# Mixer A's softmax in pairs of banks, the scaling on ScalarE, and PSUM banks by mixer

## The chip, the core and the metric

The kernel runs on one core of a Trainium2 chip. A core has a matrix engine (PE, with its weight loads shown apart as PEld), a vector engine (DVE), a scalar engine for activations (ACT), a general one (POOL) and one that only issues transfers (SP). Each works through its own queue in order. PE writes into PSUM, which has eight banks of 512 float32 per partition; DVE and ACT read it there. The metric is the device time of one execution in microseconds, the median of the runs. Times inside an execution come from the profile of one of them, counted from its first instruction.

## What is computed

One layer of a diffusion backbone on 640 tokens (128 context, 512 latent), model width 1024. Cut to what matters:

```python
h = RMSNorm(x) * (1 + scale1) + shift1
aq, ak, av, bq, bk, bv, ga, gb = split(h @ w_in)      # 34 tiles of 128 columns
# mixer A: 8 query heads, 2 key heads, all 512 latent + 128 cached keys
p = softmax(q @ k.T / 8)                              # [512 queries, 640 keys] per head
a = p @ v
# mixer B: 8 heads, a window of 384 or 512 keys per 128 queries, with a bias
b = softmax(q @ k.T / 8 + bias) @ v
x = x + gate1 * ((sigmoid(ga) * (a @ w_br_a) + sigmoid(gb) * (b @ w_br_b)) @ w_out)
x = x + gate2 * (relu(h2 @ w1) ** 2 @ w2)
```

The context queries of each mixer read the 128 context keys alone. Products are made in three parts (`wh*xh + wh*xl + wl*xh`, L339 to L341), with each operand split into a high and a low half of its bits.

## The kernel before

Feature tiles lie on the 128 partitions, tokens along the free dimension, in halves of 320. The program has stages: the first norm with the first three tiles of the input projection (to 57 us), attention of mixer A and then of mixer B with the other input tiles laid between as filler (to 345 us), then merge, output projection and MLP.

**Attention** is a list of units (L951 to L956): per pair of heads `HeadA`, `HeadA`, `CtxPair`, four times, and then the same for mixer B. `attention` (L921) goes through it in steps. A step takes one transposed key tile `T(i)` of the unit before, one score tile `S(i)` of the present unit, and the product with the values (`pv`) that the last step's `T` left. The rest of a budget of `STEP` = 2050 ns goes to the filler (`F.spend`, L875), whose pieces are three matmuls, booked at 400 ns.

- `HeadA.S` (L629) makes the scores of 128 queries and 640 keys as two products of 320 into two banks. For each DVE finds the maximum (L641); a minimum of the two negated maxima follows (L642), then two exponentials on ACT with their sums (L644), the sum of the sums (L645), a reciprocal (L618) and the scaling of the 640 columns on DVE (L619).
- `HeadA.T` (L650) transposes a key tile of the four query tiles into one bank (L653); ACT and DVE split it (L606, L607), and `pv` multiplies it with the values (L660, L661).
- `fill_tile` (L788) multiplies one input tile for the first half of the tokens and then for the second, into a bank each (`pg`), which ACT copies out (L813, or L553 for mixer B's queries). Mixer A's later queries go through a norm (L527) and a rotation.
- The weights are copied to their high part by ACT (L301), and POOL or DVE subtracts it to get the low part (L302), 128x1024 in one instruction.

**PSUM** is one pool for the whole program (L69): two banks `g` for products, three `s` for scores, two `t` for transposes, one `o` for the product with the values.

**What sets the order.** Outside of marked stretches a list scheduler places the instructions on each engine. It goes by the program's order, and where an engine has nothing ready it pulls later work ahead, as far as the tiles it needs (banks among them) are free. So the number of banks decides how much filler can run ahead.

Of the kernel before, what the change touches and what calls it, by code (L numbers as in the profile page):

```python
# [10 lines left out]
F32 = mybir.dt.float32  # L11
# [46 lines left out]
def trunk_layer(ctx: ExitStack, tc: tile.TileContext, xT, small_in, wmodA, wmodB, tabs, cacheK, cacheV, bias,  # L58
# [10 lines left out]
    pp = ctx.enter_context(tc.tile_pool(name="pp", bufs=1, space=bass.MemoryType.PSUM))  # L69
# [27 lines left out]

    def ps_g():
        return pp.tile([P, 512], F32, tag="g", bufs=2, name="pg")

    def ps_s():
        return pp.tile([P, 512], F32, tag="s", bufs=3, name="pss")

    def ps_t():
        return pp.tile([P, 512], F32, tag="t", bufs=2, name="pt")

    def ps_o():
        return pp.tile([P, 512], F32, tag="o", bufs=1, name="po")
# [94 lines left out]
    later = []                                       # work put off until the next product  # L203
# [10 lines left out]
    class Weights:  # L214
        def __init__(self):
            self.order = list(w_order())
            self.pos = {k: i for i, (k, _) in enumerate(self.order)}
            self.loads = []                              # (key, source, number of the pair's tile)
# [31 lines left out]
        def block(self, name, i):  # L250
            """one operand of the seven products, [hi | lo]"""
# [37 lines left out]
        def conv(self):  # L289
# [4 lines left out]
            else:  # L294
# [7 lines left out]
                (nc.gpsimd if key in WPOOLSET else DVE).tensor_sub(lo, st, r32(hi))  # L302
# [52 lines left out]
    def modulate(todo, rstd, h, between=None):  # L355
        """for each (dst, x, s, sh): dst = the two parts of x * s * rstd + sh"""
# [22 lines left out]
    def warm(n):  # L379
        """keeps the tensor engine's clock up while it has to wait"""  # L380
# [3 lines left out]
    def mod_product(f, q):  # L384
        """silu(c) @ w_mod for the shift and scale of feature tile f; partial sums in four column groups"""
# [34 lines left out]
    def first_gemm(f, i, part):  # L420
        """the products of h's part with one weight tile; both parts of the tile take the high part of h"""
# [105 lines left out]
    def qk_norm(raw, g, h, bank=ps_g, src=None, buf=None):  # L527
# [23 lines left out]
    def q_part(qs, e, sl, src):  # L551
        """hi of src / 8 in the head's own partitions, lo in the other ones"""
# [4 lines left out]
    def qa_part(qs, e, raw, eng):  # L557
        """the same of mixer A's queries, whose gain holds the 1 / 8"""
# [3 lines left out]
    def k_part(k, e, dst, src, eng=None):  # L562
        """own half of the stacks k[0] = [hi; hi], k[1] = [lo; lo]"""
# [4 lines left out]
    def k_both(k, e, dst, src):  # L568
        """both halves of the stacks, the other one by the engines as well"""
# [13 lines left out]
    def v_stack(raw, cvp, bank=ps_g):  # L583
        """per key tile (ctx, lat 0..3, cache): [hi 64 | lo 64] of each of the pair's heads; in two pieces"""
# [25 lines left out]
    def combine(dst, ps, n):  # L610
        """dst (64 partitions, float32) = ps[0:64] + ps[64:128]"""
# [4 lines left out]
    def normalise(p, sm):  # L616
        rc = small("rc", 1)
        DVE.reciprocal(rc, sm)  # L618
        DVE.tensor_scalar(p, p, rc, None, op0=OP.mult)  # L619

    class HeadA:
        """512 latent queries of one head of mixer A on the latent and the cached keys"""
# [6 lines left out]
        def S(self, qt):  # L629
# [4 lines left out]
            ps = [ps_s(), ps_s()]  # L634
            p = u("pa")
            n2, s2, nm, sm = small("n2"), small("s2"), small("nm", 1), small("sm", 1)
            for j in range(2):
                c = slice(P + j * HT, P + (j + 1) * HT)
                PE.matmul(ps[j][:, :HT], q, kh[:, c], start=True, stop=False)
                PE.matmul(ps[j][:, :HT], q, kl[:, c], start=False, stop=True)  # L640
                DVE.tensor_reduce(n2[:, j:j + 1], ps[j][:, :HT], axis=AX.X, op=OP.max, negate=True)  # L641
            DVE.tensor_tensor(nm, n2[:, 0:1], n2[:, 1:2], op=OP.min)  # L642
            for j in range(2):
                ACT.activation(p[:, HALVES[j]], ps[j][:, :HT], AF.Exp, bias=nm, accum_out=s2[:, j:j + 1])  # L644
            DVE.tensor_add(sm, s2[:, 0:1], s2[:, 1:2])  # L645
# [21 lines left out]
    BQ = ((P, 384, 1, 256), (P, 512, 0, 0), (384, 512, 0, 128), (512, 384, 1, 0))   # keys, width, bias tile, columns  # L667
# [704 lines left out]
```

## Time and profile before

| what | value |
|---|---|
| median of 3 runs | 1002.95 us (1001.87 to 1005.6) |
| span of the profiled execution | 1001.3 us |
| HBM traffic over the span | 104 GB/s |
| scores of mixer A, first and last start | 75.0 and 213.8 us |
| scores of mixer B, first start | 216.8 us |
| weight loads of PE busy | 91% of the span |

The profiled execution's total time is not listed beside its span. A row of a group gives the line, engine, operation, what is written and read, count, busy time, the mean of one in ns, and the idle time before with what ended it. A row of stretches gives start and end, length, and then for each engine the busy time and the number of instructions, last the clock granted to PE (1.00 is full), the transfers' share and GB/s. A row of waits gives who waited, for whom, the total, how often, and the longest.

### The profile page before, as it was taken

What the parts mean: (1) busy time and instruction counts of PE and PEld (TensorE: products, weight loads), DVE (VectorE), ACT (ScalarE), POOL (GpSimd) and SP (SyncE); (2) the same over time, 40 slices, a digit from 0 to 9 for tenths busy, and PEclk for the clock granted to TensorE, in tenths of its full rate; (3) what the DMA queues carried; (4) which work ended last, traced back from release to release, by engine and by line L of the source; (5) the groups of instructions that cost most, each with busy time, mean ns of one, the idle gap of its engine ahead of it and who ended that gap; (6) DMA issues with size and microseconds to landing.
All of it is one profiled execution on the core that took longest, in us unless ns stands there. A gap on an engine that the chain in (4) does not pass through costs nothing.

```text
span 1001.3 us, 16554 instructions
## 1 busy us (share of the span) xinstructions
PE 955.0 (95%) x6317; PEld 908.8 (91%) x6317; DVE 705.0 (70%) x1576; ACT 517.6 (52%) x1117; POOL 173.5 (17%) x154
## 2 busy tenths in 40 slices
PE   7979899999899999999999999999999999999996
PEld 5778778978889999999998899999999999999896
DVE  4479898788866789788587677778733884368644
ACT  5475676668655564654324564237611662156542
POOL 0352232212231011201132100012200220012100
PEclk9999899999999999999999899999999999999999
DMA  9942101312543455556742153212320233120302
GB/s 347 208 172 69 31 25 44 77 43 77 135 111 103 133 160 189 181 169 185 224 126 81 47 164 110 85 43 84 106 78 28 85 106 88 60 79 29 126 22 105
DMA packets 34767, 108.47 MB, mean 108 GB/s; under 512 B 4320, under 2 KB 8032, under 8 KB 34688
## 3 DMA queue, kind: packets, MB, share of 16 engines
q1 hardware_dynamic: 27072, 82.63, 26.5%
q0 software_dynamic: 6464, 23.47, 8.1%
q10 hardware_dynamic: 1152, 1.31, 0.4%
q8 instruction: 49, 0.80, 0.3%
q14 instruction: 30, 0.25, 0.1%
HBM read 99.14 MB, written 4.60 MB: 104 GB/s over the span
## 4 chain that ended last, share of the span: by engine, by line
PE 65%; DVE 15%; ACT 8%; issue 3%; DMA 1%; POOL 0%; ACTq 0%; DVEq 0%; POOLq 0%; SPq 0%
PE pg L339 7%; PE pg L340 7%; PE pg L341 7%; PE pss L340 7%; PE pss L341 7%; PE pss L339 6%; PE pt L339 4%; PE pt L341 4%; PE pt L340 4%; DVE sr L260 3%; ACT wb L280 2%; PE pt L653 1%; PE pt L710 1%; DMA wst<-w 1%; DVE n L641 1%
## 5 line engine op out<-in xcount | busy, mean ns | idle before, releaser
L301 ACT ACTIVATE wh<-wst 128x1024 fp32r<-128x1024 f32 x84 | 88.8, 1057 | 112.4 <-PE pg L340 37.9
L302 DVE TENSOR_TENSOR wl<-wst,wh 128x1024 fp32r<-128x1024 f32 x53 | 64.8, 1223 | 67.5 <-ACT wh L301 67.4
L302 POOL TENSOR_TENSOR wl<-wst,wh 128x1024 fp32r<-128x1024 f32 x31 | 75.1, 2423 | 160.0 <-ACT wh L301 151.5
L992 DVE SCALAR_TENSOR_TENSOR mt<-wmt,cb 128x512 f32<-128x512 f32 x128 | 81.4, 686 | 0.0
L281 POOL TENSOR_TENSOR wb<-wst,wb 128x512 fp32r<-128x512 f32 x24 | 31.7, 1322 | 263.4 <-ACT wb L280 226.6
L339 PE MATMUL pss<-hidh,wh 128*128 128x320 f32 x216 | 67.0, 310 | 0.7 <-ACT hidh L1143 0.7
L340 PE MATMUL pss<-hidl,wh 128*128 128x320 f32 x216 | 67.0, 310 | 0.3
L341 PE MATMUL pss<-hidh,wl 128*128 128x320 f32 x216 | 66.7, 309 | 0.0
L607 DVE TENSOR_TENSOR pl<-pt,ph 128x512 fp32r<-128x512 f32 (+2 forms) x80 | 50.5, 633 | 18.3 <-ACT ph L606 17.3
L606 ACT ACTIVATE ph<-pt 128x512 fp32r<-128x512 f32 (+2 forms) x80 | 44.2, 555 | 28.8 <-PE pt L710 11.7
L280 ACT ACTIVATE wb<-sr 128x512 fp32r<-128x512 f32 x48 | 29.8, 627 | 51.5 <-DVE sr L260 35.6
L1150 DVE TENSOR_TENSOR hidl<-rl,hidh 128x320 fp32r<-128x320 f32 x64 | 37.5, 586 | 25.2 <-ACT hidh L1143 24.6
L988 POOL DMA_DIRECT2D wmt<-wmodB x32 | 17.1, 536 | 174.6 <-DVE mt L992 108.0
L340 PE MATMUL pg<-hidl,wh 128*128 128x320 f32 x144 | 44.7, 310 | 2.2 <-DVE hidl L1150 2.2
L281 DVE TENSOR_TENSOR wb<-sr,wb 128x512 fp32r<-128x512 f32 x48 | 36.0, 755 | 14.2 <-ACT wb L280 14.1
L339 PE MATMUL pg<-hidh,wh 128*128 128x320 f32 x144 | 44.7, 310 | 0.0
L341 PE MATMUL pg<-hidh,wl 128*128 128x320 f32 x144 | 44.5, 309 | 0.0
L340 PE MATMUL pt<-hidl,wh 128*128 128x320 f32 x136 | 42.1, 310 | 1.1 <-DVE hidl L1150 1.1
L341 PE MATMUL pt<-hidh,wl 128*128 128x320 f32 x136 | 42.0, 309 | 0.0
L339 PE MATMUL pt<-hidh,wh 128*128 128x320 f32 x136 | 42.0, 309 | 0.0
L644 ACT ACTIVATE pa<-pss,nm 128x320 f32<-128x320 f32 x64 | 33.1, 522 | 17.2 <-DVE nm L642 17.0
L339 PEld LDWEIGHTS pss<-hidh,wh 128*128 128x128 f32 x216 | 40.5, 188 | 1.5 <-ACT hidh L1143 1.5
(957 smaller groups left out, 3469.9 us busy)
## 6 DMA issues: line engine op xcount, KB each, us to landing
wst<-w SPq DMA_DIRECT2D x64, 512.0 KB, 3.6
wmt<-wmodB POOLq DMA_DIRECT2D x32, 512.0 KB, 4.2
wst<-w_in SPq DMA_DIRECT2D x31, 512.0 KB, 3.6
ms<-wmodA SPq DMA_DIRECT2D x16, 512.0 KB, 8.8
x<-xT SPq DMA_DIRECT2D x16, 320.0 KB, 6.1
bt<-bias SPq DMA_DIRECT2D x16, 320.0 KB, 3.3
wst<-w_br SPq DMA_DIRECT2D x8, 512.0 KB, 4.4
wst<-w_out SPq DMA_DIRECT2D x8, 512.0 KB, 3.5
```

What stands on the lines that cost most here:

```text
L280: ACT.activation(t[:, lo4], src, AF.Copy)
L281: later.append(lambda: (nc.gpsimd if name in BLKP else DVE).tensor_sub(t[:, hi4], src, r32(t[:, lo4])))
L301: ACT.activation(hi, st, AF.Copy)
L302: (nc.gpsimd if key in WPOOLSET else DVE).tensor_sub(lo, st, r32(hi))
L339: PE.matmul(ps, wh[:, k], xh[:, sl], start=first, stop=False)
L340: PE.matmul(ps, wh[:, k], xl[:, sl], start=False, stop=False)
L341: PE.matmul(ps, wl[:, k], xh[:, sl], start=False, stop=last)
L606: ACT.activation(ph[:, :n], pt[:, :n], AF.Copy)
L607: DVE.tensor_sub(pl[:, :n], pt[:, :n], r32(ph[:, :n]))
L644: ACT.activation(p[:, HALVES[j]], ps[j][:, :HT], AF.Exp, bias=nm, accum_out=s2[:, j:j + 1])
L992: DVE.scalar_tensor_tensor(t, st[:, q * 512:(q + 1) * 512], 1.0, r32(cb[2 * q + i][:, :512]), op0=OP.mult, op1=OP.mult, accum_out=parts[:, ...
L1150: DVE.tensor_sub(dst[1][:, sl], r[:, :HT], r32(dst[0][:, sl]))
```

## The change

It has five parts.

1. **Mixer A's scores in pairs of banks.** The two products of a query tile go into one tile of two banks. One maximum over both, one exponential of 640 columns with one sum. L641, L642, L644 and L645 become L665 and L666 of the new program.
2. **The scaling by the reciprocal** moves from DVE to ACT, for mixer A and mixer B alike.
3. **Banks by mixer.** Up to the first scores and from mixer B on, banks are as before. During mixer A there are two pairs for scores, two `t`, one `o` and one `g`. The norm of mixer A's later queries and the transposes of mixer B's first value tile use `t` in that time. The pool is closed and opened anew at the two places, and before mixer B opens its own, the last `pv` of mixer A is issued.
4. **The filler stops at half tiles** during mixer A: it yields 0 after each half, and `spend` then returns with its debt kept.
5. **POOL's subtraction** of an input tile's low part is two instructions of 128x512.

```diff
+    BANKS = {"pp": {"g": 2, "s": 3, "t": 2, "o": 1}, "pa": {"S": 2, "t": 2, "o": 1, "g": 1}}
+    def open_banks(kind, name):
+        banks.close()
+        psum["p"] = banks.enter_context(tc.tile_pool(name=name, bufs=1, space=bass.MemoryType.PSUM, reuse_waits="tile"))
+        psum["n"] = BANKS[kind]
...
+    def ps_2():
+        return psum["p"].tile([P, 2, 512], F32, tag="S", bufs=2, name="pss")
     def ps_s():
-        return pp.tile([P, 512], F32, tag="s", bufs=3, name="pss")
+        return ps_("s", "pss") if "s" in psum["n"] else ps_2()[:, 0]
...
-                (nc.gpsimd if key in WPOOLSET else DVE).tensor_sub(lo, st, r32(hi))
+                if key in WPOOLSET:
+                    for ks in (slice(0, 4), slice(4, KT)) if key[0] == "in" else (slice(0, KT),):
+                        nc.gpsimd.tensor_sub(lo[:, ks], st[:, ks], r32(hi[:, ks]))
+                else:
+                    DVE.tensor_sub(lo, st, r32(hi))
...
+    def ps_x():
+        return ps_t() if "S" in psum["n"] else ps_g()
...
     def normalise(p, sm):
         rc = small("rc", 1)
         DVE.reciprocal(rc, sm)
-        DVE.tensor_scalar(p, p, rc, None, op0=OP.mult)
+        ACT.activation(p, p, AF.Copy, scale=rc)
...
-            ps = [ps_s(), ps_s()]
+            ps = ps_2()[:, :, :HT]
             p = u("pa")
-            n2, s2, nm, sm = small("n2"), small("s2"), small("nm", 1), small("sm", 1)
+            nm, sm = small("nm", 1), small("sm", 1)
             for j in range(2):
                 c = slice(P + j * HT, P + (j + 1) * HT)
-                PE.matmul(ps[j][:, :HT], q, kh[:, c], start=True, stop=False)
-                PE.matmul(ps[j][:, :HT], q, kl[:, c], start=False, stop=True)
-                DVE.tensor_reduce(n2[:, j:j + 1], ps[j][:, :HT], axis=AX.X, op=OP.max, negate=True)
-            DVE.tensor_tensor(nm, n2[:, 0:1], n2[:, 1:2], op=OP.min)
-            for j in range(2):
-                ACT.activation(p[:, HALVES[j]], ps[j][:, :HT], AF.Exp, bias=nm, accum_out=s2[:, j:j + 1])
-            DVE.tensor_add(sm, s2[:, 0:1], s2[:, 1:2])
+                PE.matmul(ps[:, j], q, kh[:, c], start=True, stop=False)
+                PE.matmul(ps[:, j], q, kl[:, c], start=False, stop=True)
+            DVE.tensor_reduce(nm, ps, axis=AX.XY, op=OP.max, negate=True)
+            ACT.activation(p.rearrange("p (a b) -> p a b", a=2), ps, AF.Exp, bias=nm, accum_out=sm)
             normalise(p, sm)
...
             F.flush(1)
+            yield 0
...
                 c = self.step()
+                if c == 0 and "S" in psum["n"]:
+                    return
...
     k_both(AK[1], 1, slice(0, NT), kraw)
+    open_banks("pa", "pa")
     F.spend(EARLY)
...
+            if isinstance(cur_u, HeadB) and "S" in psum["n"]:
+                pend()
+                pend = None
+                open_banks("pp", "pb")
```

How the scheduler then places the work is seen at three places. The first is PE's queue up to mixer A's first scores (`pss`; `pg` is the filler, `raw` the values being transposed). Before, the third half tile of the filler ends there:

```order
L339 MATMUL pg_915<-h6h_549,wh_610 128x320
L340 MATMUL pg_915<-h6l_550,wh_610 128x320
L341 MATMUL pg_915<-h6h_549,wl_611 128x320
L339 MATMUL pg_915<-h7h_592,wh_610 128x320
L340 MATMUL pg_915<-h7l_593,wh_610 128x320
L341 MATMUL pg_915<-h7h_592,wl_611 128x320
L639 MATMUL pss_745<-akh_676,qs_680 128x320
L640 MATMUL pss_745<-akl_677,qs_680 128x320
L639 MATMUL pss_746<-akh_676,qs_680 128x320
L640 MATMUL pss_746<-akl_677,qs_680 128x320
```

In the new program, from the last transpose of the values on:

```order
L618 MATMUL pt_730<-pk_74,raw_653 128x128
L360 MATMUL pg_746<-h0h_277,wh_571 128x320
L361 MATMUL pg_746<-h0l_278,wh_571 128x320
L362 MATMUL pg_746<-h0h_277,wl_572 128x320
L360 MATMUL pg_746<-h1h_314,wh_571 128x320
L361 MATMUL pg_746<-h1l_315,wh_571 128x320
L362 MATMUL pg_746<-h1h_314,wl_572 128x320
L360 MATMUL pg_746<-h2h_365,wh_571 128x320
L663 MATMUL pss_751<-akh_678,qs_682 128x320
L664 MATMUL pss_751<-akl_679,qs_682 128x320
```

Of the 72 filler matmuls that stood ahead of the first scores, 7 are left, and the filler is in its first half tile.

The second is ACT's queue where the third head's query tiles begin (`pa` the exponentials and, in L643, their scaling; `ct` the head before, `qs` and `raw` the filler, `wh` a weight tile). Before:

```order
L644 ACTIVATE pa_1278,s2_1280<-pss_1276,nm_1281 128x320
L644 ACTIVATE pa_1278,s2_1280<-pss_1277,nm_1281 128x320
L613 ACTIVATE ct_1299<-po_1296 64x128
L644 ACTIVATE pa_1336,s2_1338<-pss_1334,nm_1339 128x320
L644 ACTIVATE pa_1336,s2_1338<-pss_1335,nm_1339 128x320
L613 ACTIVATE ct_1302<-po_1296 64x128
L553 ACTIVATE qs_1392<-pg_1327 64x320
```

And now:

```order
L666 ACTIVATE pa_1196,sm_1198<-pss_1195,nm_1197 128x640
L643 ACTIVATE pa_1196<-pa_1196,rc_1205 128x640
L637 ACTIVATE ct_1238<-po_1235 64x128
L318 ACTIVATE wh_1249<-wst_1073 128x1024
L666 ACTIVATE pa_1223,sm_1225<-pss_1222,nm_1224 128x640
L637 ACTIVATE ct_1241<-po_1235 64x128
L834 ACTIVATE raw_1149<-pg_1174 128x320
L643 ACTIVATE pa_1223<-pa_1223,rc_1232 128x640
L666 ACTIVATE pa_1268,sm_1270<-pss_1267,nm_1269 128x640
```

Each query tile has one exponential and one scaling there; the scaling needs the reciprocal `rc`, which DVE makes of the exponential's sum. In 5 of mixer A's 32 query tiles it stands right behind its exponential, in the others one or two instructions lie between.

The third is PE's queue up to mixer B's first scores (`pss<-bkh`), at the end of mixer A. Before, filler stands between the last transposes, and mixer B's first scores follow:

```order
L653 MATMUL pt<-pk,pa 128x128 x2
L341 MATMUL pg<-h3h,wl 128x320
L339 MATMUL pg<-h4h,wh 128x320
L340 MATMUL pg<-h4l,wh 128x320
L341 MATMUL pg<-h4h,wl 128x320
L339 MATMUL pg<-h5h,wh 128x320
L340 MATMUL pg<-h5l,wh 128x320
L341 MATMUL pg<-h5h,wl 128x320
L339 MATMUL pg<-h6h,wh 128x320
L340 MATMUL pg<-h6l,wh 128x320
L341 MATMUL pg<-h6h,wl 128x320
L653 MATMUL pt<-pk,pa 128x128 x2
```

And now:

```order
L674 MATMUL pt_2378<-pk_74,pa_2286 128x128
L681 MATMUL po_2353<-ph_2372,vst_720 128x512
L682 MATMUL po_2353<-pl_2373,vst_720 128x512
L681 MATMUL po_2353<-ph_2383,vst_720 128x512
L682 MATMUL po_2353<-pl_2384,vst_720 128x512
L782 MATMUL pt_2403<-pk_74,pc_2329 128x128 x2
L713 MATMUL pss_2410<-bkh_1151,qs_1318 128x384
```

Mixer A ends before mixer B begins, with no filler from the eighth head's scores on. Ahead of mixer B's first scores stand 384 filler matmuls instead of 453; ahead of the scores of its fourth to seventh head the numbers are as before.

More of the change, by code (lines that the diff above doesn't have):

```diff
@@ L68, in trunk_layer @@
     hp_ = ctx.enter_context(tc.tile_pool(name="hp", bufs=1))
-    pp = ctx.enter_context(tc.tile_pool(name="pp", bufs=1, space=bass.MemoryType.PSUM))
+    banks = ExitStack()
+    ctx.callback(banks.close)
+    BANKS = {"pp": {"g": 2, "s": 3, "t": 2, "o": 1}, "pa": {"S": 2, "t": 2, "o": 1, "g": 1}}
+    psum = {}
+    def open_banks(kind, name):
+        banks.close()
+        psum["p"] = banks.enter_context(tc.tile_pool(name=name, bufs=1, space=bass.MemoryType.PSUM, reuse_waits="tile"))
+        psum["n"] = BANKS[kind]
+    open_banks("pp", "pp")
     phase = ExitStack()
@@ L525, in kt_tile, with qk_norm @@
         return kp.tile([P, 896], F32R, tag="k", bufs=8, name=name)
-    def qk_norm(raw, g, h, bank=ps_g, src=None, buf=None):
+    def ps_x():
+        return ps_t() if "S" in psum["n"] else ps_g()
+    def qk_norm(raw, g, h, bank=ps_x, src=None, buf=None):
         sl = HALVES[h]
@@ L581, in v_cols, with v_stack @@
         return vv[:, :, 0:64], vv[:, :, 64:P]
-    def v_stack(raw, cvp, bank=ps_g):
+    def v_stack(raw, cvp, bank=ps_x):
         v = kp.tile([P, 6 * 256], F32R, tag="V", bufs=2, name="vst")
```

8 lines of the change are left out of this document (5 added, 3 removed).

## The prediction

> **What bounds the kernel now.** I read the page first, then busy time by stretch, then the waits of PE's weight loads.
>
> ```profile
> span 1001.3 us, 16554 instructions
> PE 955.0 (95%) x6317; PEld 908.8 (91%) x6317; DVE 705.0 (70%) x1576; ACT 517.6 (52%) x1117; POOL 173.5 (17%) x154
> ```
>
> PE looks saturated, but that share is an average. I cut the span where the work changes: 56.6 (last matmul of the first norm), 75.0 (mixer A's first scores), 216.8 (mixer B's first scores), 345.0 (last transposes of attention).
>
> ```profile
> 350.00:400.00 50.00, 50.00 (x342) 49.79 (x341) 44.51 (x107) 26.76 (x52) 6.91 (x13) 1.00 0.54 173
> ...
> 56.60:75.00 18.40, 14.10 (x87) 12.49 (x85) 13.85 (x22) 15.99 (x39) 9.51 (x7) 0.94 0.57 204
> 75.00:216.80 141.80, 130.44 (x770) 113.89 (x771) 118.02 (x302) 92.62 (x251) 36.11 (x25) 0.95 0.18 47
> 216.80:345.00 128.20, 122.29 (x790) 111.27 (x790) 95.30 (x275) 80.28 (x201) 25.73 (x24) 1.00 0.39 107
> 345.00:1001.00 656.00, 639.26 (x4300) 633.19 (x4298) 449.57 (x914) 301.81 (x576) 87.26 (x79) 0.99 0.34 107
> ```
>
> The columns are stretch, length, then PE, PEld, DVE, ACT, POOL busy. In 350 to 400 the weight loads fill all but 0.2 of 50 us: 342 matmuls at 0.146 us each, nothing to gain. So PEld is the meter for work, and what it leaves idle is stall: 5.9 us before the first scores, **27.9 us in mixer A**, 16.9 us in mixer B. In mixer A the busiest engine is DVE, 118.0 of 141.8 us (83%); ACT has 92.6.
>
> ```profile
> PEld pss L639 <- ACT pa L644: 8.2, 13, 2.0
> PEld pss L639 <- POOL qs L560: 5.9, 2, 4.5
> PEld pt L653 <- DVE pa L619: 5.0, 9, 1.0
> PEld pt L653 <- DVE pl L607: 1.6, 1, 1.6
> PEld pg L339 <- ACT raw L813: 1.5, 3, 0.7
> ```
>
> These are PE's waits in mixer A. The scores wait 8.2 us for a bank that the exponentials hold, the transposes 5.0 us for DVE's scaling. Both are what the change touches.
>
> The sum below is against the profiled execution, span 1001.3. Its total time is not listed apart; the median of the runs is 1002.95, so 1.65 us lie around the span if this was a median run, and I add the gain to 1002.95.
>
> **Part 1: the stretch before the first scores.** The one filler bank and the later pool take the cover away: 72 filler matmuls stood ahead of the first scores, now 7 do. The trace has the same 72, 381 and 465 in the three stretches: this row for one of the three lines of a product, and the other two have equal counts.
>
> ```profile
> 56.60:75.00 18.40, 7.50 (x24) 4.42 (x24) 0.94 0.57 204
> 75.00:216.80 141.80, 41.97 (x127) 24.79 (x127) 0.95 0.18 47
> 216.80:345.00 128.20, 49.28 (x155) 29.25 (x155) 1.00 0.39 107
> ```
>
> 65 x 0.146 = 9.5 us of PE work leave a stretch in which PE waits anyway; they must be paid later. The start itself hangs on this:
>
> ```profile
> 70.55 2.80 POOL L302 TENSOR_TENSOR wl<-wst,wh 128x1024 fp32r<-128x1024 f32 x1 [2.44 <-ACT wh L301]
> 73.43 3.15 POOL L560 TENSOR_TENSOR qs<-raw,qs 64x640 fp32r<-64x640 f32 x2
> ...
> 71.18 1.49 ACT L559 ACTIVATE qs<-raw 64x640 fp32r<-64x640 f32 x2 [0.19 <-DVE raw L546]
> ...
> 75.01 0.64 PE L639 MATMUL pss<-akh,qs 128*128 128x320 f32 x1 [4.23 <-POOL qs L560]
> ```
>
> The first query half is on ACT until 71.92, but POOL is in a weight subtraction until 73.35. In the new order POOL's query work stands ahead of that subtraction: 71.92 + 1.57 = 73.5, so the scores start **1.5 us earlier** (ends: 0, if DVE's two-input work holds POOL, and 1.5). Before them PE idled 4.2 us and will idle longer; the matmul after the idle took 0.64 us, and I leave the slow spell after it as it was (0 to 2 us more).
>
> **Part 2: mixer A.** DVE's and ACT's rows for its 32 query tiles:
>
> ```profile
> L641 DVE TENSOR_REDUCE n<-pss 128x1 f32<-128x320 f32 x64 | 30.8, 483 | 7.1 <-PE pss L640 6.9
> L619 DVE TENSOR_SCALAR pa<-pa,rc 128x640 f32<-128x640 f32 x31 | 17.1, 551 | 0.2
> L642 DVE TENSOR_TENSOR nm<-n 128x1 f32<-128x1 f32 x32 | 10.1, 315 | 0.1
> L645 DVE TENSOR_TENSOR sm<-s 128x1 f32<-128x1 f32 x31 | 8.4, 272 | 5.3 <-ACT pa L644 5.0
> L618 DVE RECIPROCAL rc<-sm 128x1 f32<-128x1 f32 x31 | 4.9, 157 | 0.4
> ...
> L644 ACT ACTIVATE pa<-pss,nm 128x320 f32<-128x320 f32 x64 | 33.1, 522 | 17.2 <-DVE nm L642 17.0
> L301 ACT ACTIVATE wh<-wst 128x1024 fp32r<-128x1024 f32 x8 | 8.5, 1062 | 2.1 <-PE pg L340 1.8 <-issue 0.3
> L813 ACT ACTIVATE raw<-pg 128x320 f32<-128x320 f32 x11 | 4.6, 433 | 1.5 <-PE pg L341 1.5
> L559 ACT ACTIVATE qs<-raw 64x640 fp32r<-64x640 f32 x6 | 4.4, 735 | 3.2 <-DVE raw L546 3.1
> ...
> 170.55 1.14 ACT pa L644 x4
> ```
>
> DVE: the 640-wide maximum is not in the trace. Between 0.48 (one of 320) and 0.97 (two) I take 0.82, one plus the 320 elements at 1.04 ns: 32 x 0.82 = 26.2 instead of 30.8. The minimum, the sum and the scaling go: 10.1 + 8.4 + 17.1. DVE falls by 40 us to about 78. The means of 315 and 272 ns are long for one element, and this is why:
>
> ```profile
> 128.77 2.46 POOL L302 TENSOR_TENSOR wl<-wst,wh 128x1024 fp32r<-128x1024 f32 x1 [20.10 <-ACT wh L301]
> ...
> 128.93 2.32 DVE L642 TENSOR_TENSOR nm<-n 128x1 f32<-128x1 f32 x1
> 131.17 0.68 DVE L607 TENSOR_TENSOR pl<-pt,ph 128x512 fp32r<-128x512 f32 x1
> ```
>
> A DVE operation of one element sat from 128.93 until POOL was done. Both kinds that were caught so are removed; the halved subtraction lets DVE in between for the rest. POOL does the same elements (0 to 0.2 us more each, hidden: POOL is busy 36 of 142 us).
>
> ACT: two exponentials with their accumulator reads take 1.14 us end to end. One of 640 is one of 320 (0.522) plus 320 elements at 0.77 ns, the slope from 735 ns at 640 to 1062 at 1024 being 0.85; I take 0.79 plus 0.1 of the read, 0.89 (ends 0.72 and 1.14). That saves 32 x 0.25 = 8.0. The scaling of 640 is new there: nearest is the 64x640 copy, 735 ns (ends 0.55, DVE's time, and 1.06, the 1024-wide copy): 32 x 0.74 = 23.7. Work of the last head that ran past 216.8 adds some 3, and where the scaling stands right behind its own exponential, 5 of 32 times, ACT waits some 0.35 for DVE's reciprocal (0.16 and the rest of the read): 1.8. ACT: 92.6 - 8.0 + 23.7 + 3 + 1.8 = **113 us**. Behind a waiting scaling ACT holds the next exponential, the copies of the transposes and the filler's eviction, and PE waits for all three.
>
> The Trainium skill, page "ScalarE: Activation LUTs", section "Rules for kernel authors", says to put a multiply on VectorE and not on ScalarE. The trace agrees on the price, 551 ns on DVE against 735 for the nearest ACT row. The same page's section on what a table load costs gives 186 ns + 0.833 per element + about 93 for a pointer operand, 812 ns here; by that ACT would have 2.5 us more.
>
> PE: 377 filler matmuls instead of 381, plus what this row shows missing.
>
> ```profile
> L653 PE MATMUL pt<-pk,pa 128*128 128x128 f32 x146 | 26.9, 287 | 3.9 <-DVE pa L619 2.4 <-DVE pl L607 1.4
> L661 PE MATMUL po<-pl,vst 128*128 128x512 f32 x35 | 15.3, 438 | 0.1
> ...
> 127.88 0.60 PE L653 MATMUL pt<-pk,pa 128*128 128x128 f32 x4
> 128.23 0.40 PE L640 MATMUL pss<-akl,qs 128*128 128x320 f32 x1
> ```
>
> 14 transposes of 160 and 10 of 80 products came after 216.8; the order now closes mixer A first. At 0.09 us each (four in 0.35) and 0.146 x 512 / 320 = 0.235: 14 x 0.09 + 10 x 0.235 = 3.6, so 113.9 - 0.6 + 3.6 = **116.9 us**. Three engines are thus at 117, 113 and 78 where they were at 114, 93 and 118. Of the 27.9 us idle I take away the bank waits (8.2; two whole pairs of banks), the scaling waits (5.0) and 1.4 of the wait for POOL (5.9 less the 4.5 before 75.0). Idle left: 13.3, length 130.2, **11.6 us less**. The ends: 117, PE without a gap, and 140, if the busiest engine again fills only 83% (116.9 / 0.83). The single filler bank is inside this: each half tile must wait for its eviction, 14 times 0.43 at most, but the filler now pauses there and scores or transposes stand in between.
>
> **Part 3: mixer B and after.** 528 filler matmuls instead of 465 (counted to its last transposes, 912 - 384 and 918 - 453, by the order): 63 x 0.146 = 9.2, less the 3.6 that went to mixer A: 5.6 more. The scaling moves here too:
>
> ```profile
> L619 DVE TENSOR_SCALAR pb<-pb,rc 128x384 f32<-128x384 f32 x16 | 8.9, 557 | 0.2
> L619 DVE TENSOR_SCALAR pb<-pb,rc 128x512 f32<-128x512 f32 x16 | 7.7, 483 | 0.1
> L606 ACT ACTIVATE ph<-pt 128x384 fp32r<-128x384 f32 x14 | 6.9, 490 | 6.6 <-PE pt L710 6.6
> L565 ACT ACTIVATE bkh<-raw 64x512 fp32r<-64x512 f32 x4 | 2.5, 626 | 0.0
> ```
>
> DVE loses 16.6 of 95.3; ACT gets 16 x 0.49 + 16 x 0.63 = 17.9 and stands at 98 of 128, with 12 of 32 scalings right behind their exponential. DVE's relief and ACT's waits pull against each other; I take 2 us more (ends -5 and +6). Mixer B: **7.6 us more**. After 345 the work is the same and PE full: 0.
>
> **Sum:** -1.5 - 11.6 + 7.6 = -5.5, so 1002.95 - 5.5 = **997.4 us**. Attention would end near 339.5 instead of 345. Break-even is a mixer A of 135.7 us.
>
> **Rivals.**
> 1. *ScalarE becomes the bound (slower).* Place: each query tile, exponential, reciprocal on DVE, scaling. If DVE has a split of 0.68 us (the row above) queued ahead of most reciprocals, ACT waits 0.8 instead of 0.35, also in the 27 cases with another instruction between: 32 x 0.8 = 26, ACT at 137 in mixer A, which then takes 142 or more. -1.5 + 0 + 7.6 and 4 more in mixer B: 1013. It decides from 135.7 us on. For: ACT gains 24 us there, and its order is exponential, one instruction, scaling. Against: DVE falls to 78 and is seldom busy. It is also where the Trainium skill's rule above points.
> 2. *What A saves, B pays (no change).* Mixer A at 134 to 138 since PE lacks filler while the last head and a half run, where the order shows none: about 1003.
> 3. *Everything flows (faster).* With DVE unloaded PE runs nearly without gaps: A at 119, B's idle down by 5: -1.5 - 22.8 + 0.6, so 979.
>
> **Chances.** Forecast (990 to 1002) 0.5; rival 1 0.2; rival 2 0.15; rival 3 0.15. A measurement of this kernel tells about 0.5% (5 us) from nothing. Faster by more: 0.31 of the forecast's 0.5, all of rival 3: 0.46. Slower by more: rival 1 and a little: 0.21. Between: 0.33. The range that leaves 2 in 10 out is 984 to 1011.
>
> **What would show it.** First scores near 73.5; PEld idle before them up from 5.9 to about 14; the new scaling at 0.7 to 0.8 us on ACT; mixer B's first scores near 204 (at 209 or later the forecast fails and rival 1 or 2 holds); no small DVE operation of 2 us in mixer A; scores hardly waiting for banks; the stretch from mixer B's first scores to the end of attention at 136. If ACT's own waits for the reciprocal are over 10 us in mixer A, rival 1's mechanism is at work.

## The result, and the profile after

The changed kernel takes **1010.19 us** (median of 4 runs, 1009.27 to 1011.22) against 1003.45 for the kernel before on the same chip: ratio 1.0057, 95% interval 1.0029 to 1.0084. It is some 0.6% slower, where 997.4 was forecast. The profiled execution took 1011.02 us, so 1.8 us lie around its span.

The head of the changed kernel's page, and its busy time by stretch. The stretches run from the last matmul of the first norm to the first scores of mixer A, then by pairs of heads (query heads 1 and 2, and so on) to mixer B's first scores, to the last transposes of attention, and to the end. The columns are those of the prediction.

```profile
span 1009.2 us, 16426 instructions
...
PE 955.4 (95%) x6317; PEld 912.2 (90%) x6317; DVE 659.0 (65%) x1416; ACT 550.7 (55%) x1117; POOL 176.0 (17%) x173
```

```profile
57.87:75.32 17.45, 5.28 (x23) 2.83 (x21) 12.96 (x24) 12.96 (x32) 7.53 (x7) 0.76 0.57 210
75.32:114.20 38.88, 37.28 (x226) 34.40 (x226) 24.84 (x49) 29.14 (x60) 11.26 (x11) 0.93 0.21 53
114.20:145.40 31.20, 27.79 (x173) 24.43 (x173) 21.28 (x44) 27.55 (x58) 8.15 (x6) 1.00 0.11 35
145.40:179.70 34.30, 33.60 (x210) 31.41 (x211) 17.69 (x37) 24.24 (x49) 10.31 (x8) 0.95 0.11 33
179.70:222.68 42.98, 35.77 (x186) 28.53 (x185) 25.66 (x53) 31.37 (x67) 7.64 (x9) 0.88 0.21 56
222.68:353.16 130.48, 127.85 (x844) 119.95 (x843) 78.94 (x236) 97.54 (x228) 28.89 (x32) 1.00 0.38 108
353.16:1009.20 656.04, 637.46 (x4290) 631.48 (x4288) 449.22 (x911) 300.96 (x573) 87.27 (x79) 0.99 0.33 106
```

The same cut of the kernel before, from mixer A's first scores on. (The prediction set the end of attention at 345.0 by eye; its last transposes start at 347.17, which is used here for all kernels.)

```profile
75.01:104.10 29.09, 26.61 (x149) 22.82 (x149) 26.73 (x72) 17.53 (x49) 7.82 (x8) 0.92 0.24 61
104.10:143.40 39.30, 35.35 (x202) 30.59 (x203) 32.71 (x83) 26.52 (x73) 8.52 (x6) 0.91 0.12 34
143.40:179.00 35.60, 32.62 (x205) 28.54 (x204) 29.77 (x75) 24.57 (x66) 10.30 (x6) 1.00 0.11 32
179.00:216.82 37.82, 35.87 (x220) 31.95 (x219) 28.82 (x75) 24.02 (x67) 9.46 (x7) 0.95 0.26 65
216.82:347.17 130.35, 124.44 (x804) 113.24 (x804) 97.42 (x278) 81.46 (x203) 25.73 (x24) 1.00 0.39 107
```

Length less PEld's busy time is what weight loads idle. Mixer A went from 141.8 to 147.4 us, and its idle time from 27.9 to 28.6: nothing was gained there. But it moved. Heads 1 to 6 idle 14.1 us instead of 22.0; the last pair idles **14.5 instead of 5.9**, at a granted clock of 0.88. Mixer B does 6.7 us more work in the same time: its idle time fell from 17.1 to 10.5. DVE's load in mixer A fell from 118.0 to 89.5 (78 forecast), and ACT's is 112 (113 forecast).

The engines' prices are about what was forecast. ACT's and DVE's groups in mixer A of the changed kernel (count, busy us, mean ns, and the idle time before them with what ended it):

```profile
L643 ACT ACTIVATE pa<-pa,rc 128x640 f32<-128x640 f32 x32 | 26.5, 830 | 1.4 <-DVE rc L642 1.4
L666 ACT ACTIVATE pa<-pss,nm 128x640 f32<-128x640 f32 x32 | 25.3, 791 | 6.1 <-DVE nm L665 5.7
```

```profile
L665 DVE TENSOR_REDUCE nm<-pss 128x1 f32<-128x640 f32 x32 | 26.0, 811 | 7.4 <-PE pss L664 7.3
```

PE's waits in mixer A of the changed kernel, longest first (10.0 of the first row is the idle time ahead of the first scores):

```profile
PEld pss L663 <- POOL qs L584: 12.8, 3, 10.0
PEld pss L663 <- ACT pa L666: 4.0, 6, 1.4
PEld po L682 <- DVE pl L631: 3.0, 6, 0.9
PEld po L681 <- ACT ph L630: 2.7, 4, 1.7
PEld po L681 <- DVE ao L638: 1.8, 3, 0.8
PEld pt L674 <- ACT pa L643: 1.7, 3, 0.8
```

The two waits that the change was aimed at did shrink, scores for banks from 8.2 to 4.0 and transposes for the scaling from 5.0 to 1.7. In their place stand waits of the value products (`po`) for the split of the transposes (L630, L631), 5.7 us, of which there were 1.4 before.

### The profile page after: what moved, and what is told of

Its sections match the earlier page's. It is cut to its first block, busy times and chain, and to the rows that moved or that the text cites. A ratio compares the mean times of both kernels' runs of the same rounds, so it can differ in the third digit from the quotient of the medians.

```text
span 1009.2 us, 16426 instructions
## 1 busy us (share of the span) xinstructions
PE 955.4 (95%) x6317; PEld 912.2 (90%) x6317; DVE 659.0 (65%) x1416; ACT 550.7 (55%) x1117; POOL 176.0 (17%) x173
## 4 chain that ended last, share of the span: by engine, by line
PE 59%; ACT 15%; DVE 13%; issue 5%; DMA 1%; POOL 1%; ACTq 0%; DVEq 0%; POOLq 0%; SPq 0%
PE pg L360 7%; PE pg L361 7%; PE pg L362 7%; PE pss L361 7%; PE pss L362 6%; PE pss L360 6%; PE pt L360 4%; PE pt L361 4%; PE pt L362 4%; DVE sr L277 4%; ACT wb L297 3%; ACT pb L720 1%; ACT pa L666 1%; ACT wh L318 1%; ACT pa L643 1%
## 5 line engine op out<-in xcount | busy, mean ns | idle before, releaser
L321 POOL TENSOR_TENSOR wl<-wst,wh 128x512 fp32r<-128x512 f32 (+1 forms) x50 | 76.8, 1549 | 170.5 <-ACT wh L318 161.7
L631 DVE TENSOR_TENSOR pl<-pt,ph 128x512 fp32r<-128x512 f32 (+2 forms) x80 | 50.6, 635 | 40.3 <-ACT ph L630 39.3
L630 ACT ACTIVATE ph<-pt 128x512 fp32r<-128x512 f32 (+2 forms) x80 | 44.0, 552 | 26.2 <-PE pt L674 14.1
L361 PEld LDWEIGHTS pss<-hidl,wh 128*128 128x128 f32 x216 | 40.5, 188 | 1.0 <-DVE hidl L1179 1.0
```

The source lines that it names most:

```text
L321: nc.gpsimd.tensor_sub(lo[:, ks], st[:, ks], r32(hi[:, ks]))
L361: PE.matmul(ps, wh[:, k], xl[:, sl], start=False, stop=False)
L630: ACT.activation(ph[:, :n], pt[:, :n], AF.Copy)
L631: DVE.tensor_sub(pl[:, :n], pt[:, :n], r32(ph[:, :n]))
```

## The experiments

Ratios are to the kernel before on the same chip (the changed kernel: 1.0057), with 95% intervals; differences between kernels are taken from the ratios, at 1003.5 us.

| kernel | median us | ratio | 95% |
|---|---|---|---|
| e1 gate tile in A | 1003.04 | 0.9987 | 0.9969 to 1.0005 |
| e2 start covered | 995.20 | 0.9909 | 0.9881 to 0.9936 |
| e3 both | 998.52 | 0.9939 | 0.9916 to 0.9961 |
| e4 scaling on DVE | 1014.71 | 1.0102 | 1.0074 to 1.0129 |
| e5 e2 with 96 matmuls | 1001.98 | 0.9976 | 0.9957 to 0.9995 |
| e6 e2, scaling on DVE | 1001.54 | 0.9973 | 0.9958 to 0.9988 |
| e7 e2, POOL whole | 996.01 | 0.9918 | 0.9896 to 0.9940 |
| e8 before, scaling on ACT | 1006.68 | 1.0024 | 1.0012 to 1.0036 |
| e9 e2, spread | 1000.93 | 0.9969 | 0.9953 to 0.9985 |
| e10 spread | 1014.35 | 1.0103 | 1.0079 to 1.0128 |
| e11 e2, two gate tiles in A | 998.41 | 0.9954 | 0.9935 to 0.9974 |
| e12 e2, no stop | 1002.30 | 0.9982 | 0.9963 to 1.0000 |
| e13 before, pool reopened at A | 1004.23 | 1.0010 | 0.9995 to 1.0026 |
| e14 before, pool reopened at B | 1021.06 | 1.0169 | 1.0144 to 1.0193 |
| e15 before, both | 1022.84 | 1.0183 | 1.0158 to 1.0208 |
| e16 before, stop | 1001.90 | 0.9985 | 0.9972 to 0.9998 |
| e17 second switch later | 1003.60 | 0.9993 | 0.9978 to 1.0007 |
| e18 e2, second switch later | **988.95** | **0.9843** | 0.9817 to 0.9869 |

**First, the filler's place and the scaling's engine (e1 to e4).** e1 moves a gate tile between the lists, e2 spends filler before the pool is switched, e3 does both, e4 undoes the scaling.

```diff
-AFILL = (1, 10, 2, 6, 3, 14, 21)
+AFILL = (1, 10, 2, 6, 3, 14, 21, 29)
-BFILL = (11, 7, 15, 12, 8, 16, 13, 9, 17, 29, 22, 30)
+BFILL = (11, 7, 15, 12, 8, 16, 13, 9, 17, 22, 30)
```

```diff
-    open_banks("pa", "pa")
-    F.spend(EARLY)
+    F.spend(9600)
+    open_banks("pa", "pa")
```

```diff
-        ACT.activation(p, p, AF.Copy, scale=rc)
+        DVE.tensor_scalar(p, p, rc, None, op0=OP.mult)
```

> The changed kernel, with one gate tile moved from mixer B's list to mixer A's: by the order 480 filler matmuls stand before the end of mixer A instead of 384, and the last two heads have 72 and 24 more of them. Theory 'cover' (the gain was lost because the last head and a half of mixer A run without filler, 14.5 us of idle weight loads in the last head pair): the 96 matmuls, 14 us of work, go into that idle time, mixer A grows by 2 to 5 us, the time from mixer B's first scores to the end of attention falls by 12 to 14; in all 8 to 11 us less than the changed kernel, 999 to 1002. Theory 'ScalarE' (ACT is 7.6 of 8 us busy in the filler-free tail and stays the bound whatever PE does): the same matmuls fit beside it, but each eviction and score queues behind ACT; mixer A grows by 8 or more, in all 0 to 4 us less, 1006 to 1010.

> The changed kernel, with the first filler run spent before the bank pools are switched: 72 filler matmuls stand ahead of the first scores again instead of 7; all 384 of mixer A's are then used up by the end of its sixth head. Theory 'cover': the idle time before the first scores falls from 13 to about 4 us, but the same 65 matmuls are missing at the end of mixer A, where two heads then run bare: mixer A 137 to 141 us long, in all 1004 to 1010. Theory 'start' (the lost gain is the stretch before the first scores, and the half-speed clock after its idle time): the 9.5 us come back in full, 999 to 1002. Theory 'ScalarE': as the cover theory, 1006 to 1010.

> Both edits at once: 72 filler matmuls ahead of the first scores and 480 before the end of mixer A; its last head still runs bare. Theory 'cover': the two gains add, as filler now covers the start and all but one head: 16 to 20 us less than the changed kernel, 990 to 995, ahead of the kernel before. Theory 'ScalarE': 3 to 6 us less, 1004 to 1007. If mixer B, with 438 matmuls left instead of 528, runs short of filler in its turn, its idle time shows it (10.5 us now) and the sum ends near 1000.

> The changed kernel with the scaling back on VectorE (pairs, bank pools, filler stop and halved subtraction stay): ACT loses 26.5 us in mixer A and about 18 in mixer B, DVE gains 17.6 and 16.6. The filler's places are the same. Theory 'cover': the idle time of the start and the tail stays, within 3 us of the changed kernel, 1007 to 1013. Theory 'ScalarE': the tail, where ACT is full, loses its 0.83 us for each of eight tiles and mixer A's other pairs their waits for exponentials: 5 us or more less, below 1005.

e1 is 7 us below the changed kernel, a little above the cover theory's range: filler in the bare tail brings half of its 14 us. e4 is 4.5 us above the changed kernel: the scaling on ScalarE helps, and the ScalarE theory falls. e2 is the surprise: 15 us back for 65 matmuls, 9.5 us of work, moved ahead of the first scores. Its mixer A:

```profile
75.04:99.40 24.36, 24.22 (x144) 22.60 (x145) 19.77 (x38) 20.50 (x40) 10.60 (x10) 0.90 0.27 82
99.40:141.60 42.20, 40.69 (x260) 37.01 (x259) 26.03 (x55) 34.79 (x77) 11.31 (x9) 1.00 0.13 40
141.60:172.70 31.10, 30.04 (x192) 26.89 (x191) 19.75 (x40) 25.82 (x52) 11.27 (x9) 1.00 0.17 50
172.70:205.74 33.04, 26.48 (x136) 18.98 (x136) 24.37 (x52) 27.79 (x60) 2.11 (x4) 0.95 0.16 42
```

130.7 us, and PE idles 1.8 us in the first pair: there PE itself sets the pace, and filler put there costs its whole length. The changed kernel has 64 more weight loads in mixer A than e2. They make 9.3 us at 0.146, but the loads are busy 13.3 us more, at a lower granted clock (0.95 and 0.88 in the last two pairs, 1.00 and 0.95 in e2), and idle 3.4 us more. The last pair, without any filler, still idles 14.1. e3's gains do not add: its extra filler lands in heads 5 to 7, its last head is still bare, mixer A is 13.4 us longer than e2's, and mixer B, which gave the filler, only 8.9 us shorter.

**Second, the same start with one part undone each, and the scaling alone (e5 to e8).** e5 spends 12800 instead of 9600 ahead of the switch; e6 is e2 with e4's edit; e7 is e2 with `for ks in (slice(0, KT),)`, the whole subtraction; e8 is the kernel before with the scaling line of the change.

> e2 with 96 filler matmuls ahead of the first scores instead of 72: 24 x 0.146 = 3.5 us of work go into the 4.45 us that PE still idles there, and the spell of half-speed matmuls behind that idle time (75.0 to 79.9 in e2, 0.267 us from one matmul to the next instead of 0.147) should shorten or go, worth up to 2.2 us. Theory 'start' (what counts is the work hidden ahead of the first scores): 3.5 to 5.7 us less than e2, 989 to 992. Theory 'tail' (what leaves the tail is given back there: filler ends one head earlier, and two and a half heads run bare at 16.5 us each): 0 to 1 us less than e2, 994 to 996.

> e2 with the scaling back on VectorE, so that with the start filled again the scaling is judged by itself. Theory 'start': the scaling on ScalarE helps, by the 4.5 us that e4 lost against the changed kernel, or a little less: 998 to 1001. Theory 'ScalarE' (the scaling hurts, and only the bare start hid that): 990 or below.

> e2 with the whole subtraction on POOL (2.4 to 2.8 us each) instead of two halves. By the order nothing else moves on PE. If the halves free VectorE's small operations, e2's gain holds some of it: 1 to 3 us more than e2, 996 to 998, and reciprocals of 2 us show up on DVE. If, with the minimum and the sum gone, nothing small is left to be caught, no difference: 994 to 996.

> The kernel before with nothing changed but the scaling, now on ScalarE (single banks, two maxima, two exponentials, 72 filler matmuls ahead of the first scores). DVE loses 17.1 us in mixer A and 16.6 in mixer B, ACT gains 26.5 and 18: 92.6 + 26.5 = 119 of 141.8 in mixer A. If the scaling on ScalarE is worth what e4 says: 4 to 5 us less than before, ratio 0.995. If ACT without the merged exponentials is too full for it: same or slower, ratio 1.000 to 1.005; then the pairs are what makes room for it.

e6 loses 6.4 us, e7 nothing that can be told, and e8 is 2.4 us slower than the kernel before: the scaling on ScalarE pays beside the rest of the change and not without it. That the merged exponentials make the room for it was the expectation; no run adds them alone. e5 missed both expectations, 6.7 us above e2. Its PE timeline ahead of the first scores (start, duration, idle before and who ended it) shows why:

```profile
72.79 1.44 PE L558 MATMUL pg<-qsq,pk 128*128 128x320 f32 x2 [2.91 <-ACT qsq L556]
73.56 0.94 PE L360 MATMUL pg<-h0h,wh 128*128 128x320 f32 x1
74.29 0.47 PE L361 MATMUL pg<-h0l,wh 128*128 128x320 f32 x1
```

The fourth half tile stands in PE's queue behind a query norm of the filler, which waits for ACT. It starts at half speed at 73.56 and ends at 78.5, so the scores come 22.7 us after the norm instead of 18.7. In the profiled execution, 3.6 us longer than e2's, that is the whole difference: mixer A is as long as e2's with 24 filler matmuls fewer. Filler covers a wait only if it can run when the wait begins.

**Third, spreading the filler, more of it, and the stop (e9 to e12).** e9 (on e2) and e10 (on the changed kernel) give mixer A's steps a budget of 1700 instead of 2050; e11 is e2 with tiles 29 and 22 in A's list; e12 is e2 without the `return` at a half tile.

```diff
-                F.spend(max(0, STEP - t))
+                F.spend(max(0, (1700 if "S" in psum["n"] else STEP) - t))
```

> e2 with a smaller filler budget for each step of mixer A (1700 ns instead of 2050; mixer B keeps 2050). The same 384 matmuls, the same 72 ahead of the first scores, but by the order the last two heads get 12 and 12 of the last 72 between them and sit beside 72 in all, where e2's last two have none. Theory 'bare heads' (a head without filler leaves PE idle, 14.1 us of e2's mixer A stand in its last head pair): that idle time falls by 6 to 8 us, the pairs before it get shorter by the work they lose, 987 to 990. Theory 'chain' (PE, ScalarE and VectorE pass each tile on in turn, and the chain sets the pace with filler or without): what the last pair wins, the others lose, 994 to 997.

> The changed kernel with the smaller filler budget in mixer A and nothing else: 7 matmuls ahead of the first scores as in the changed kernel, the last head gets 32. Theory 'bare heads': the last head pair's idle time falls from 14.5 to about 7 us and its half-speed spells go, 1000 to 1004. Theory 'chain': 1008 to 1011.

> e2 with two gate tiles moved from mixer B to mixer A: 576 matmuls before the end of mixer A, so that no head is bare (the last one has 48); mixer B keeps 350. e3 had one tile less, and its last head was bare. Theory 'bare heads': mixer A's idle time falls from 25.2 to 18 or less, and mixer B stays at about 11: 988 to 992. If mixer B, with a third of its filler gone, idles more by what mixer A saves: 995 to 999.

> e2 without the filler's stop at half tiles. By the order the filler differs by a half tile here and there, no more. Expected: no difference from e2 beyond 2 us, 994 to 997. Were the single filler bank a cost that the stop avoids, filler matmuls would wait for evictions: half tiles at 0.43 us each, up to 4 us more, 999.

All four are slower than their base, and e9, e10 and e12 fit neither expectation. e11 is in its second range; its last head is no longer bare: mixer A's idle time is 19.0 us, but mixer B, with less filler, idles 15.0 (10.7 in e2). Both together that is 1.9 us less than in e2, so idle time does not explain the 4.5 us; the profiled execution, the shortest of e11's eight, does not show them (937.1 us from the first norm on, e2's 937.3). Without the stop e12 loses 7.3 us, and its idle time in mixer A is 30.6 instead of 25.2. PE's waits in e12's mixer A:

```profile
PEld po L681 <- ACT ph L630: 6.3, 7, 2.1
PEld pt L674 <- ACT pa L643: 5.4, 7, 1.1
...
PEld pg L360 <- ACT raw L834: 1.1, 4, 0.5
```

The filler's own wait for its bank is only 1.1 us (1.2 in e2), so PE does not lose the time there; the chain's waits grew. Why spread filler is worse was not settled. Longer pieces do not explain it: the longest unbroken piece of filler from mixer A's first scores on is 32 matmuls in e10 against 24 in the changed kernel, but 21 in e9 against 24 in e2.

**Fourth, the pools alone, in the kernel before (e13 to e16).** The pool is closed and opened again with the same banks and the changed kernel's `reuse_waits="tile"`, at mixer A (e13), ahead of mixer B (e14) and at both (e15). e16 is the kernel before with the stop, in both mixers.

```diff
+    open_banks("pa")
     F.spend(EARLY)
...
+            if isinstance(cur_u, HeadB) and cur_u.hd == 0:
+                pend()
+                pend = None
+                open_banks("pb")
```

> The kernel before, with nothing changed but its bank pool closed and opened again, with the same banks, where the changed kernel opens mixer A's pool. By the order that alone takes the filler away ahead of the first scores: 7 matmuls instead of 72, as in the changed kernel; from its third head on the order is the old one. Theory 'cover' (the pool's place, not the pairs, ScalarE or the single bank, took the time at the start): the 65 matmuls, 9.5 us, come back in mixer A, and the idle time before the first scores rises from 6 to 14.6 us: 8 to 14 us more than before, ratio 1.008 to 1.014. Theory 'work only moved' (mixer A, with 27.9 us of idle weight loads, takes the 65 matmuls into its idle time): 0 to 4 us more, ratio 1.000 to 1.004.

> The kernel before, with its pool closed and opened again, with the same banks, ahead of mixer B, after mixer A's last products, as in the changed kernel. By the order the last head and a half of mixer A run without filler (384 matmuls to the end of mixer A instead of 481), and mixer B gets what they lose. Theory 'cover': idle weight loads in the last head pair rise from 5.9 to about 14 us as in the changed kernel, mixer B's fall from 17 to about 11, in all 0 to 5 us more, ratio 1.000 to 1.005. Theory 'bare heads cost all' (the whole 8.5 us, with nothing back in mixer B): ratio 1.008 or more.

> Both pools reopened in the kernel before: the filler's places are the changed kernel's, 7 ahead of the first scores and 384 to the end of mixer A, with the old banks, two maxima, two exponentials, and the scaling on VectorE. Theory 'cover': the two costs add to 8 to 18 us more than before, 1012 to 1021, so that the changed kernel at 1010 is faster than this one by 2 to 10 us: that is what its pairs, its scaling and its stop are worth. If the rest of the change costs something of its own, this kernel is faster than the changed one, below 1010.

> The kernel before with the filler's stop at half tiles, in both mixers, and its two filler banks. e12 lost 7 us without the stop where there is one filler bank. If the stop is worth something for itself (filler in whole half tiles, not in pieces), 2 us or more less than before, ratio below 0.998; if it only makes up for the single bank, no difference, 0.998 to 1.002.

This turned my account round: I had expected the cost at the start. e13 costs 1.0 us, which can't be told from nothing, and e14 costs **17.0**, the second theory each time. e13's mixer A:

```profile
75.18:114.70 39.52, 37.51 (x226) 33.66 (x226) 31.62 (x81) 25.84 (x68) 11.00 (x9) 0.96 0.19 52
114.70:145.10 30.40, 29.85 (x190) 26.86 (x190) 24.88 (x72) 21.25 (x60) 7.93 (x4) 1.00 0.10 36
145.10:180.80 35.70, 32.72 (x205) 28.58 (x204) 29.86 (x75) 24.70 (x66) 10.35 (x6) 1.00 0.11 32
180.80:217.03 36.23, 34.30 (x221) 30.67 (x218) 28.71 (x75) 24.14 (x67) 9.45 (x7) 1.00 0.25 68
```

The start idles 14.5 us as in the changed kernel, but mixer A is as long as before, 141.85 us: its idle time takes the 65 matmuls in (27.9 down to 22.1, and the granted clock in its pairs is 0.96 to 1.00, before 0.91 to 1.00). e14's last pair of heads and mixer B:

```profile
180.50:226.67 46.17, 36.39 (x177) 28.31 (x176) 31.23 (x84) 26.32 (x73) 7.37 (x7) 0.82 0.20 52
226.67:363.66 136.99, 129.56 (x849) 120.05 (x848) 95.86 (x268) 80.50 (x196) 27.63 (x24) 1.00 0.36 103
```

The pair idles 17.9 us (5.9 before) at a clock of 0.82, and mixer B gets 6.8 us more work without losing idle time. No bank count, pair, exponential or engine differs from the kernel before: this edit alone costs that. It does two things, it closes the pool and issues the last products ahead of the next stage's scores; which of the two weighs more was not separated, here or in e17 and e18. e15 at 1.0183 says what the rest of the change is worth with the same places: 12.6 us *less*. e16 gains 1.5 us (0.2 to 2.8): in the kernel before the stop is worth little.

**Last, the second switch in the changed kernel (e17, e18).** Mixer B's first two heads stay in mixer A's pool; e18 has e2's start too.

```diff
-            if isinstance(cur_u, HeadB) and "S" in psum["n"]:
+            if isinstance(cur_u, HeadB) and cur_u.hd >= 2 and "S" in psum["n"]:
```

> The changed kernel with its second switch of pools two heads later: mixer B's first two heads still run in the paired banks with one filler bank. By the order the last head and a half of mixer A get 48 filler matmuls (432 at its last product instead of 384), 7 ahead of the first scores as in the changed kernel. Theory 'switch' (e14: closing the pool ahead of mixer B costs 17 us in the kernel before, most of it idle and half-speed PE time in the bare heads): the last head pair's idle time falls from 14.4 to 8 or less, its clock goes back to 1.0, 998 to 1004. Theory 'pace' (with the pairs, PE sets mixer A's pace, so filler there costs what it is long, and two heads of mixer B with one filler bank lose what is left): 1007 to 1011.

> e2 (72 filler matmuls ahead of the first scores) with the second switch two heads later: 24 filler matmuls stand in the last head and a half where e2 has none. Theory 'switch': the idle time of the last head pair falls from 14.1 to about 10, 989 to 993, the fastest so far. Theory 'pace' (e3, e9 and e11 had filler there and were 3 to 6 us slower than e2): 996 to 1001.

The switch theory held both times, with more idle time gone in e18 than it said (4.9 us left, not 10): 6.4 us from the changed kernel to e17, 6.6 from e2 to e18. e17's last pair and mixer B, then e18's mixer A and B:

```profile
179.20:211.09 31.89, 29.39 (x184) 25.45 (x184) 19.75 (x41) 25.64 (x54) 6.62 (x7) 1.00 0.22 61
211.09:345.45 134.36, 131.04 (x845) 119.42 (x844) 84.68 (x250) 102.79 (x242) 29.89 (x34) 1.00 0.38 108
```

```profile
76.53:100.90 24.37, 24.30 (x144) 22.82 (x145) 19.80 (x38) 20.50 (x40) 10.61 (x10) 0.89 0.27 81
100.90:143.10 42.20, 40.67 (x261) 36.92 (x260) 26.06 (x55) 34.79 (x77) 11.30 (x9) 1.00 0.14 40
143.10:174.20 31.10, 30.58 (x199) 27.86 (x198) 19.76 (x40) 25.82 (x52) 11.29 (x9) 1.00 0.17 51
174.20:198.01 23.81, 22.38 (x141) 18.89 (x139) 19.77 (x42) 23.09 (x51) 1.59 (x3) 1.00 0.12 38
198.01:331.15 133.14, 129.45 (x834) 117.58 (x833) 83.54 (x246) 101.56 (x238) 29.39 (x33) 1.00 0.39 109
```

The last pair's idle time is 6.4 and 4.9 us at full clock. Mixer B pays some back, 14.9 and 15.6 idle instead of 10.5 and 10.7. **e18, at 988.95 us, is faster than both kernels**: ratio 0.9843 to the kernel before. The two places as a square, in us:

| | both switches as changed | second one later | start covered (e2) | both (e18) |
|---|---|---|---|---|
| changed kernel | 1010.2 | 1003.6 | 995.2 | 989.0 |
| mixer A: length | 147.4 | 134.7 | 130.7 | 121.5 |
| mixer A: weight loads idle | 28.6 | 20.9 | 25.2 | 15.0 |

The start is worth 15 us and the later second switch 6.5, whichever comes first.

## Why the prediction was wrong

By its terms, in the profiled executions. **Start, -1.5:** -1.1, right (17.45 us from the norm's last matmul to the first scores, 18.52 before). Up to that matmul the profiled execution took 1.4 us more, which no term has. **After attention, 0:** +1.9; this stretch is 654.5 us in e9 and 657.5 in e5, with the same number of matmuls, so 1.9 can be chance. **Mixer B, +7.6:** +0.1. The extra work came (6.7 us, 5.6 forecast), but I took 2 us more idle time and 6.6 went. Mixer B's idle time is 12.5 us in e4, with the scaling on DVE, and 16.9 in e14, where POOL's subtraction is whole too, so DVE's relief had more to give than ACT's waits took; the two parts were not separated in mixer B. Mixer B came out 7.5 us better than forecast, which hid part of the next miss.

**Mixer A, -11.6: measured +5.6. This is the step that failed**, and within it "Of the 27.9 us idle I take away the bank waits (8.2), the scaling waits (5.0) and 1.4 of the wait for POOL ... Idle left: 13.3". The work was near the forecast (118.8, forecast 116.9); the idle time was 28.6, and mixer B's first scores came at 222.7, past the 209 that the prediction named as a sign of failing. The subtraction itself was nearly right: in e18, where the filler stands around the chain again, 15.0 us are left of 27.9. What it left out is what the pools do to the cover. I booked 65 matmuls out of the start, and 63 more into mixer B, each at its own length, and took the idle time beside them as unchanged. Moved alone in the kernel before, the second switch costs 17.0 us (e14); in the changed kernel putting it two heads later returns 6.5. The 65 matmuls were booked at 9.5 us and cost 15 (e2). In the kernel before mixer A swallowed them (e13, +1.0). The likely reason is that the relief takes from the same idle time that would have taken them in: heads 1 to 6 idle 22.0 us in the kernel before and 11.2 in e2. That is argued from kernels side by side, not shown by a run of its own.

DVE's 78 us in mixer A came out at 89.5 for another reason: the prediction took 40 us of rows off the busy time, but a group's rows overlap their neighbours'. The rows listed for DVE there add up to some 134 us before, where it is busy 118.0, and to some 97 after.

**Rival 2** had half of the mechanism ("PE lacks filler while the last head and a half run") and the wrong size: mixer A at 134 to 138, and mixer B paying. Its chance of 0.15 was too small, since the order showed the bare heads. No rival had the start, which is worth more. **Rival 1** had nearly the right time, 1013, for the wrong reason. ACT waits 1.4 us for the reciprocal in all of mixer A, not 26, and taking the scaling off ScalarE makes it slower (e4, e6). **ScalarE's price** was low: 830 ns for 740. The Trainium skill's estimate that the prediction quoted, 812 (page "ScalarE: Activation LUTs", the section on what a table load costs), is nearer. Its rule to put a multiply on VectorE (same page, "Rules for kernel authors") goes the other way from these runs: 551 ns on DVE against 830 on ACT, and still 4.5 and 6.4 us better on ACT; in the kernel before it is 2.4 us worse there (e8). Which engine is fuller does not decide it: in mixer A of the kernel before DVE has 118.0 us and ACT 92.6, and moving the work off DVE was no gain; in e6 they have 105.9 and 87.6, and it is. The reason stays open.

Of the change's parts, then: the scaling -4.5 to -6.4 beside the rest; the stop -7.3 in e2; the halved subtraction nothing by itself; all but the pools' switches together -12.6 (e15 against the changed kernel); the switches +18.4 in the kernel before. The pairs were not undone alone. The change did what it says on the engines, and lost it, with 5.7 us more, where its pools open and close.

## What to carry to other kernels

Filler is a fixed stock: before a wait is counted as gain, look in the order at what filler stands beside it after the change. A matmul that leaves a covered wait can cost more than its length where it arrives, or next to nothing if idle time there takes it in: the same 65 cost 15 us in one kernel and 1.0 in the other. Closing a pool between two stages, with the last products issued first, ended their overlap here and cost 17.0 us; move such a switch alone in the old kernel before anything else is blamed. Two savings that draw on the same idle time need not add.

## What the runs showed of the hardware

Half-speed spells of TensorE after short pauses. The idle time ahead of mixer A's first scores (10.0 us in the changed kernel's waits) is followed by half-speed matmuls, as the prediction saw before: from 75.32 to 80.56 the granted clock is 0.50, and matmuls of 320 columns follow each other every 0.27 us instead of 0.15. In the changed kernel's bare tail much shorter pauses did the same (PE's timeline):

```profile
195.47 0.31 PE L663 MATMUL pss<-akh,qs 128*128 128x320 f32 x1
195.62 0.31 PE L664 MATMUL pss<-akl,qs 128*128 128x320 f32 x1
...
197.30 0.38 PE L789 MATMUL po<-ph,vst 128*128 128x256 f32 x1 [1.12 <-DVE ao L638]
...
199.20 0.44 PE L674 MATMUL pt<-pk,pa 128*128 128x128 f32 x2 [0.57 <-ACT pa L643]
200.15 0.60 PE L663 MATMUL pss<-akh,qs 128*128 128x320 f32 x1 [0.52 <-issue]
200.56 0.47 PE L664 MATMUL pss<-akl,qs 128*128 128x320 f32 x1
200.82 0.47 PE L663 MATMUL pss<-akh,qs 128*128 128x320 f32 x1
```

From 200.56 on scores follow each other every 0.26 us instead of 0.15, after pauses of 1.12, 0.57 and 0.52 us, 2.2 in all within 4 us. The granted clock is 1.00 from 196.2 to 200.1, where PE is busy 1.8 of 3.9 us, and 0.56 from 200.1 to 204.0. The Trainium skill (page "TensorE: Matmul & The Clock Gate", Part 1) says that the clock halves after an idle window of about 3.4 us that runs freely; no single pause here was that long, so the row fits it only if such a window counts as idle when PE is merely busy too little. So a bare tail costs twice here: 14 us of idle time, and half speed on part of its work (clock 0.88 over the last pair).
